# The second pass of the attention scores as two 64-row matmuls on different halves of the rows, with a second copy of the keys' high part

## The chip, the cores and the metric

The kernel runs on one core of a Trainium2 chip, in one launch. The metric is the device time of one execution in microseconds (us), as the median of several; less is better. The engines are named as in the profile: PE does matmuls (PEld its weight loads), DVE, ACT and POOL do elementwise work, and SP issues nearly all DMAs.

## The reference

One layer of a hybrid sequence model on 2048 tokens of width 1024. All three head groups read one projection of RMSNorm(x); their outputs are gated, concatenated, projected back and added to x, and a last RMSNorm follows. The change touches the first group, six heads of softmax attention over a band of nine 64-token chunks:

```python
scores = jnp.einsum('bnqhd,bnkhd->bnhqk', qc, kb).astype(jnp.float32) * (d ** -0.5)
...
scores = jnp.where(valid[None, :, None, None, :], scores + bias[None, None], NEG)
p = jax.nn.softmax(scores, axis=-1).astype(v.dtype)
o = jnp.einsum('bnhqk,bnkhd->bnqhd', p, vb)
```

Here d is 64. The second group is an mLSTM and the third a gated linear attention (GLA), both chunk by chunk with a carried state.

## The kernel before

**Numbers in two parts.** A float32 matmul operand is split into a high part, its value rounded to the type float32r, and a low part, the rest. A product is then made of float32r matmuls: high with high, high with low, low with high.

**Two stages.** Stage A goes through the tokens in four blocks of 512 (`q` = 0 to 3, `QT` = 512): projections (lines 243 to 245 and 263 to 265), mLSTM and GLA, and queries, keys and values of the attention written to DRAM (`q_d`, `k_d`, `v_d`) with the high and the low part side by side. Stage B, from `with ExitStack() as pb_` on, does the attention and the output projection for the same four blocks. The last few projections of stage A (`proj_kept`) are kept back and run in stage B, mixed with the attention of block 0. Then `load_wo` loads the output weights into the room that the projection weights leave, and from block 1 on the attention of block q is mixed with the output projection (`out_mm`, lines 945 to 947) of block q-1.

**Scores.** For each head, `scores` loads `qq` (L809, two DMAs: the queries' high and low part, each copied to rows 0 to 63 and to rows 64 to 127 of the 128 partitions, which are the rows of PE's array), `kk` (L812: the keys' high part on rows 0 to 63 and their low part on rows 64 to 127) and `vv` (L814). It then goes through four tiles of 128 queries (`tt`). A tile sees up to 640 keys, in at most two segments: up to 384 keys, and the last 256. Each segment has a PSUM bank of its own (`s`, two banks in all). L826 makes two passes over the segments: pass 0 multiplies the queries' high part, on both halves of the rows, with the whole of `kk`, and pass 1 the queries' low part in the same way. In block 0 the first two tiles have one segment only, and the others 128+256 and 256+256 keys; in blocks 1 to 3 every tile has 384+256. DVE reads a segment out of PSUM, adds the bias table `bt` or the mask `mz` and takes the minimum (L840), ACT does the exponential (L843), and POOL scales (L845).

**Mix.** `mix` transposes the probabilities on PE (L887), splits them (L892 on ACT, L893 on DVE), multiplies with `vv` (L901, L904), collects two heads in `cc` (L908 ACT, L909 DVE), multiplies with the gate `gt` (L921 POOL; loaded at L862) and splits the product (L852 ACT, L853 POOL).

**What sets the order.** PE's order is the order in which the code is written, as `merge` and `spread` interleave it. The other engines' and SP's order is set by the framework's scheduler. Each engine, and SP for its DMAs, takes its instructions in that order. A tile lives in a pool, at a fixed address; a tile in room that another tile used waits until that one's last reader and writer are done. The pool `early` of stage B lies at the right end of the on-chip memory. It holds `bt`, `bc`, `mz`, two `qq` and two `kk`, in this order from low to high addresses. It is opened after stage A's right-hand pools are closed, in room that these used. `bt` is loaded (L773), lowered by `bc` for each of the six heads (L777, POOL, six instructions) and partly overwritten (L778, POOL).

**Other 64-row matmuls.** Stage A has matmuls on 64 rows already: L522 multiplies six heads' keys with their queries in plain float32, the even heads on rows 0 to 63 and the odd ones on rows 64 to 127, into different banks. A plain float32 matmul is two instructions in the profile. The profile gives the part of the array that an instruction uses, rows*columns: 128*128 is the whole, 64*128 one half of the rows, 128*64 and 128*32 a part of the columns.

Of the kernel before, what the change touches and what calls it, by code (L numbers as in the profile page):

```python
# [8 lines left out]
FP32 = mybir.dt.float32  # L9
FR = mybir.dt.float32r  # L10
# [6 lines left out]
P = 128  # L17
D = 1024
KT = D // P
QT = 512  # L20
# [79 lines left out]
def f32(ap):  # L100
    return ap.bitcast(FP32)
# [3 lines left out]
def trunk_kernel(ctx: ExitStack, tc: tile.TileContext, xT, x, w_f, w_t, w_o, w_gates, norm_g, conv_w,  # L105
                 gate_sel, one_row, bias, ml_g, gla_g, final_g, out):
    nc = tc.nc
# [6 lines left out]
    k_d = dram.tile([AH, 2, 64, S], FP32, name="k_d")  # L114
# [27 lines left out]
    with ExitStack() as pa_:  # L142
# [3 lines left out]
        big = pa_.enter_context(tc.tile_pool(name="big", bufs=2, side="right"))  # L146
# [616 lines left out]
    with ExitStack() as pb_:  # L763
        psum = pb_.enter_context(tc.tile_pool(name="psumb", bufs=2, space=PSUM, reuse_waits="tile"))
        early = pb_.enter_context(tc.tile_pool(name="early", bufs=2, side="right", reuse_waits="tile"))
        big = pb_.enter_context(tc.tile_pool(name="bbig", bufs=2, side="right", reuse_waits="tile"))
        one = early

        def pbank(tag):
            return (psum_i if tag == "ip" else psum).tile([P, 512], FP32, name=tag)  # L770
# [29 lines left out]
        cur = {}  # L800

        def scores(q, h, out_):
            dma = nc.sync
            kb = max(0, q * QT - 512)
            nk = (q + 1) * QT - kb
            qq = early.tile([P, 2, QT], FR, name="qq")
            for r in range(2):
                a = h % 2
                dma.dma_start(f32(qq[64 * r:64 * r + 64]),  # L809
                                  q_d[h // 2, :, 64 * a:64 * a + 64, q * QT:(q + 1) * QT].rearrange("l d t -> d l t"))  # L810
            kk = early.tile([P, 1024], FR, name="kk")
            dma.dma_start(f32(kk[:, :nk]), k_d[h, :, :, kb:kb + nk].rearrange("l d t -> (l d) t"))  # L812
            vv = big.tile([P, 8, P], FR, name="vv", bufs=3)
            dma.dma_start(f32(vv[:, :nk // P, :]), v_d[h, kb:kb + nk, :].rearrange("(b p) d -> p b d", p=P))  # L814
            pts, pair = [], []
            for tt in range(NC):
                i = NC * q + tt
                k0 = max(0, i * P - 512)
                n = (i + 1) * P - k0
                ko = k0 - kb  # L820
                nA = max(0, n - 256)
                segs = ([(0, nA)] if nA else []) + [(nA, n - nA)]
                sps = [pbank("s") for _ in segs]
                for l in range(2):
                    for sp, (c0, cn) in zip(sps, segs):
                        nc.tensor.matmul(sp[:, :cn], qq[:, l, tt * P:(tt + 1) * P], kk[:, ko + c0:ko + c0 + cn],  # L826
                                         start=(l == 0), stop=(l == 1))
                if q == 0:
                    if tt < 2:
                        pair.append(big.tile([P, 640], FP32, name="pt", bufs=8))  # L830
                    pt = pair[(0, 1, 1, 0)[tt]]
                    pt = pt[:, (512, 384, 0, 0)[tt]:][:, 0:n]
                else:
                    pt = big.tile([P, 640], FP32, name="pt", bufs=8)
                sm = big.tile([P, 4], FP32, name="sm", bufs=8)
                init = -NEG
                for a, (sp, (c0, cn)) in enumerate(zip(sps, segs)):
                    last = a == len(segs) - 1
                    in1 = bt[:, h, 256 - cn:256] if last else mz[:, 384 - cn:384]
                    nc.vector.tensor_tensor_reduce(out=pt[:, c0:c0 + cn], in0=sp[:, :cn], in1=in1, scale=-1.0, scalar=init,  # L840
                                                   op0=ALU.add, op1=ALU.min, accum_out=sm[:, a:a + 1])
                    init = sm[:, a:a + 1]
                nc.scalar.activation(pt[:, :n], pt[:, :n], AF.Exp, bias=init, scale=-1.0, accum_out=sm[:, 2:3])  # L843
                nc.vector.reciprocal(sm[:, 3:4], sm[:, 2:3])  # L844
                nc.gpsimd.tensor_scalar(pt[:, :n], pt[:, :n], sm[:, 3:4], 0.5, op0=ALU.mult, op1=ALU.mult)  # L845
                pts.append((pt, ko // P, n // P))
                yield
            out_.append((vv, pts, nk // P))

        def split_y(src, k):  # L850
            yk = (big if k < 3 else late["p"]).tile([P, 2, QT], FR, name="y", bufs=6 if k < 3 else 5)
            nc.scalar.copy(yk[:, 0, :], src)  # L852
            nc.gpsimd.tensor_tensor(yk[:, 1, :], src, f32(yk[:, 0, :]), op=ALU.subtract)  # L853
            return yk

        def mix(q, h, Y, vv, pts, nkb):
            mr = slice(64 * (h % 2), 64 * (h % 2) + 64)
            cr = slice(64 - 64 * (h % 2), 128 - 64 * (h % 2))
            if h % 2 == 0:
                cur["cc"] = big.tile([P, QT], FP32, name="cc")  # L860
                cur["gt"] = big.tile([P, QT], FP32, name="gt")
                nc.sync.dma_start(cur["gt"], ga_d[:, h // 2, q * QT:(q + 1) * QT])  # L862
            cc, gt = cur["cc"], cur["gt"]
            todo = []
            for pr in range(NC // 2):
                pp = pts[2 * pr:2 * pr + 2]
                one_use, two_use = [], []
                for b in range(nkb):
                    use = tuple(tt for tt in range(2) if pp[tt][1] <= b < pp[tt][1] + pp[tt][2])
                    if use:  # L870
                        (one_use if len(use) == 1 else two_use).append((b, use))
                packs, width = [], 1024
                for b, use in one_use + two_use:
                    if width + P * len(use) > 512:
                        packs.append([])
                        width = 0
                    packs[-1].append((b, use, width))
                    width += P * len(use)
                todo += [(pr, pp, g, pk, g == len(packs) - 1) for g, pk in enumerate(packs)]
            ops = {}  # L880

            def turn_(pr, pp, g, pk, last):
                tp = pbank("tp")
                for b, use, w in pk:
                    for x_, tt in enumerate(use):
                        pt, b0, _ = pp[tt]
                        nc.tensor.transpose(out=tp[:, w + x_ * P:w + (x_ + 1) * P],  # L887
                                            in_=pt[:, (b - b0) * P:(b - b0 + 1) * P], identity=ident)
                wd = pk[-1][2] + P * len(pk[-1][1])
                ph = big.tile([P, 512], FR, name="ph", bufs=3)  # L890
                pl = big.tile([P, 512], FR, name="pl", bufs=3)
                nc.scalar.copy(ph[:, :wd], tp[:, :wd])  # L892
                nc.vector.tensor_tensor(pl[:, :wd], tp[:, :wd], f32(ph[:, :wd]), op=ALU.subtract)  # L893
                return ph, pl

            def pv(pr, pp, g, pk, last, ph, pl):
                if g == 0:
                    ops[pr] = pbank("w")
                op = ops[pr]
                for e, (b, use, w) in enumerate(pk):  # L900
                    nc.tensor.matmul(op[:, use[0] * P:use[0] * P + P * len(use)], vv[:, b, :], ph[:, w:w + P * len(use)],  # L901
                                     start=(g == 0 and e == 0), stop=False, skip_group_check=True)
                for e, (b, use, w) in enumerate(pk):
                    nc.tensor.matmul(op[0:64, use[0] * P:use[0] * P + P * len(use)], vv[:, b, 64 * (h % 2):64 * (h % 2) + 64],  # L904
                                     pl[:, w:w + P * len(use)], start=False, stop=(last and e == len(pk) - 1), skip_group_check=True)
                if last:
                    ps_ = slice(pr * ST, (pr + 1) * ST)
                    nc.scalar.copy(cc[mr, ps_], op[cr, :ST])  # L908
                    nc.vector.tensor_tensor(cc[mr, ps_], op[mr, :ST], cc[mr, ps_], op=ALU.add)  # L909

            held = []
            for it in todo:
                ph, pl = turn_(*it)
                yield
                if held:
                    pv(*held.pop())
                    yield
                held.append(it + (ph, pl))
            pv(*held.pop())
            if h % 2 == 1:  # L920
                nc.gpsimd.tensor_tensor(cc, cc, gt, op=ALU.mult)  # L921
                Y[h // 2] = split_y(cc, h // 2)
            yield
# [148 lines left out]
```

## Time and profile before

| | |
|---|---|
| median of 3 runs | 1430.01 us (1427.89 to 1431.16) |
| the profiled execution | 1430.58 us, of which 1428.9 us from its first to its last instruction |
| PE's mean granted clock | 0.953 of full speed |
| stage B | from 1005 us to the end |
| L826, all 360 matmuls | 80.8 us busy, 333 ns each as recorded |
| DMA traffic | 180.10 MB, 126 GB/s in the mean |

The rows that the argument rests on stand in the prediction. In a timeline row the first number is the start of the first instruction in us, the second the time from there to the end of the last one, and xN their number; [..] is idle time before it and who ended it. PE starts an instruction while those ahead of it still run, so what one costs is read from start to start and not from its recorded duration.

### The profile page before, as it was taken

What the parts mean: (1) busy time and instruction counts of PE and PEld (TensorE: products, weight loads), DVE (VectorE), ACT (ScalarE), POOL (GpSimd) and SP (SyncE); (2) the same over time, 40 slices, a digit from 0 to 9 for tenths busy, and PEclk for the clock granted to TensorE, in tenths of its full rate; (3) what the DMA queues carried; (4) which work ended last, traced back from release to release, by engine and by line L of the source; (5) the groups of instructions that cost most, each with busy time, mean ns of one, the idle gap of its engine ahead of it and who ended that gap; (6) DMA issues with size and microseconds to landing.
All of it is one profiled execution on the core that took longest, in us unless ns stands there. A gap on an engine that the chain in (4) does not pass through costs nothing.

```text
span 1428.9 us, 20086 instructions
## 1 busy us (share of the span) xinstructions
PE 1319.6 (92%) x7044; PEld 1064.9 (75%) x7044; DVE 788.7 (55%) x1874; ACT 616.5 (43%) x1173; POOL 606.5 (42%) x847
## 2 busy tenths in 40 slices
PE   5899989989998998999899899998878999999997
PEld 2678768867877876888677677787756887877876
DVE  6525556662664765265566527556556756656731
ACT  5634313463432347343224534321456555655531
POOL 4215762322576222266622325651245354454452
PEclk7999989999999999999999999997877999999999
DMA  7433214453421445432244533231587464555322
GB/s 245 152 112 117 74 54 131 133 177 111 118 74 56 130 140 177 125 111 74 67 124 121 156 118 93 73 110 49 148 241 229 130 184 133 179 161 160 99 67 89
DMA packets 107205, 180.10 MB, mean 126 GB/s; under 512 B 9824, under 2 KB 54752, under 8 KB 107104
## 3 DMA queue, kind: packets, MB, share of 16 engines
q1 hardware_dynamic: 102496, 170.43, 40.4%
q10 hardware_dynamic: 4608, 8.39, 1.6%
q8 instruction: 56, 0.92, 0.3%
q14 instruction: 45, 0.37, 0.1%
HBM read 143.14 MB, written 35.65 MB: 125 GB/s over the span
## 4 chain that ended last, share of the span: by engine, by line
PE 67%; DVE 12%; ACT 8%; DMA 6%; issue 4%; POOL 3%; SPq 0%; POOLq 0%; ACTq 0%; DVEq 0%
PE ip L243 11%; PE ip L245 10%; PE ip L244 10%; PE s L826 3%; PE ip L947 3%; PE ip L946 3%; PE ip L945 3%; PE ip L263 3%; PE ip L264 3%; PE ip L265 3%; PE tp L887 2%; DVE pt L840 2%; PE ga L673 2%; ACT w L235 2%; DVE qk L449 2%
## 5 line engine op out<-in xcount | busy, mean ns | idle before, releaser
L243 PE MATMUL ip<-x,w 128*128 128x512 f32 x800 | 326.7, 408 | 0.0
L244 PE MATMUL ip<-x,w 128*128 128x512 f32 x800 | 313.3, 392 | 1.2 <-DVE x L324 1.2
L245 PE MATMUL ip<-x,w 128*128 128x512 f32 x800 | 313.6, 392 | 0.0
L235 ACT CAST w<-wraw 128x1024 fp32r<-128x1024 f32 x132 | 138.3, 1049 | 193.9 <-PE ip L245 136.4
L236 DVE TENSOR_TENSOR w<-wraw,w 128x1024 fp32r<-128x1024 f32 x88 | 114.2, 1299 | 172.1 <-ACT w L235 170.0
L236 POOL TENSOR_TENSOR w<-wraw,w 128x1024 fp32r<-128x1024 f32 x44 | 106.1, 2410 | 217.5 <-ACT w L235 217.3
L243 PEld LDWEIGHTS ip<-x,w 128*128 128x128 f32 x800 | 150.9, 189 | 43.8 <-issue 11.9
L244 PEld LDWEIGHTS ip<-x,w 128*128 128x128 f32 x800 | 151.1, 189 | 32.8 <-DVE x L324 2.9
L245 PEld LDWEIGHTS ip<-x,w 128*128 128x128 f32 x800 | 150.7, 188 | 33.0
L845 POOL TENSOR_SCALAR pt<-pt,sm 128x640 f32<-128x640 f32 (+2 forms) x96 | 70.4, 735 | 148.8 <-DVE sm L844 118.1
L263 PE MATMUL ip<-w,x 128*128 128x512 f32 x256 | 105.5, 412 | 20.8 <-ACT zg L423 14.4
L264 PE MATMUL ip<-w,x 128*128 128x512 f32 x256 | 104.1, 407 | 4.6 <-POOL w L236 3.8
L945 PE MATMUL ip<-wo,y 128*128 128x512 f32 x256 | 107.0, 418 | 0.0
L843 ACT ACTIVATE pt<-pt,sm 128x640 f32<-128x640 f32 (+2 forms) x96 | 73.3, 764 | 71.0 <-DVE sm L840 68.0
L265 PE MATMUL ip<-w,x 128*128 128x512 f32 x256 | 103.3, 403 | 0.0
L947 PE MATMUL ip<-wo,y 128*128 128x512 f32 x256 | 101.7, 397 | 0.3 <-POOL y L853 0.3
L946 PE MATMUL ip<-wo,y 128*128 128x512 f32 x256 | 101.5, 396 | 0.0
L893 DVE TENSOR_TENSOR pl<-tp,ph 128x512 fp32r<-128x512 f32 (+2 forms) x126 | 74.6, 599 | 31.5 <-ACT ph L892 30.4
L826 PE MATMUL s<-kk,qq 128*128 128x384 f32 (+1 forms) x360 | 80.8, 333 | 10.7 <-DVE sm L840 9.2
L826 PEld LDWEIGHTS s<-kk,qq 128*128 128x128 f32 x360 | 60.6, 201 | 29.9 <-DVE sm L840 23.4
L633 POOL TENSOR_TENSOR prd<-gk,zg 128x16 f32<-128x16 f32 (+15 forms) x128 | 66.5, 520 | 33.4 <-PE pw L639 26.5
L892 ACT CAST ph<-tp 128x512 fp32r<-128x512 f32 (+2 forms) x126 | 63.1, 509 | 33.6 <-PE tp L887 32.4
(240 smaller groups left out, 2418.8 us busy)
## 6 DMA issues: line engine op xcount, KB each, us to landing
wraw<-in_w_f SPq DMA_DIRECT2D x100, 512.0 KB, 3.6
wraw<-in_w_t SPq DMA_DIRECT2D x32, 512.0 KB, 4.2
qq<-q_d SPq DMA_DIRECT2D x48, 256.0 KB, 4.5
kk<-k_d SPq DMA_DIRECT2D x18, 512.0 KB, 6.4
vv<-v_d SPq DMA_DIRECT2D x18, 512.0 KB, 7.3
xraw<-in_x SPq DMA_DIRECT2D x16, 512.0 KB, 4.6
xraw<-in_xT SPq DMA_DIRECT2D x16, 512.0 KB, 7.5
xr<-in_x SPq DMA_DIRECT2D x16, 512.0 KB, 3.7
```

Source lines behind the costliest of these rows:

```text
L235: nc.scalar.copy(w[:, :, 0, :], rv)
L236: other().tensor_tensor(w[:, :, 1, :], rv, f32(w[:, :, 0, :]), op=ALU.subtract)
L243: nc.tensor.matmul(ps, w[:, k, 0, :], X[k][:, 0, :], start=(k == 0), stop=False)
L244: nc.tensor.matmul(ps, w[:, k, 0, :], X[k][:, 1, :], start=False, stop=False)
L245: nc.tensor.matmul(ps, w[:, k, 1, :], X[k][:, 0, :], start=False, stop=(k == KT - 1))
L263: nc.tensor.matmul(ps, X[k][:, 0, t], w[:, 0, :], start=(k == 0), stop=False)
L264: nc.tensor.matmul(ps, X[k][:, 0, t], w[:, 1, :], start=False, stop=False)
L265: nc.tensor.matmul(ps, X[k][:, 1, t], w[:, 0, :], start=False, stop=(k == KT - 1))
L826: nc.tensor.matmul(sp[:, :cn], qq[:, l, tt * P:(tt + 1) * P], kk[:, ko + c0:ko + c0 + cn], start=(l == 0), stop=(l == 1))
L945: nc.tensor.matmul(ps, Y[k][:, 0, t], wo[k, j][:, 0, :], start=(e == 0), stop=False)
L946: nc.tensor.matmul(ps, Y[k][:, 0, t], wo[k, j][:, 1, :], start=False, stop=False)
L947: nc.tensor.matmul(ps, Y[k][:, 1, t], wo[k, j][:, 0, :], start=False, stop=(e == KT - 1))
```

## The change

`scores` loads a second copy of the keys' high part, `k2`, on rows 64 to 127 (L815), for the last 640 keys (512 in block 0). Pass 0 stays as it was (L829). In pass 1 (L833) only the keys' high part is multiplied with the queries' low part: the product of the two low parts is no longer made. The first segment uses rows 0 to 63 (`qq` and `kk`), the last segment rows 64 to 127 (`qq` and `k2`); a tile with one segment uses rows 64 to 127. `cc` and `gt` have one buffer each where they had two. Lines behind the change stand six lines further on than before (L840 is now L846, L945 is L951).

```diff
             kk = early.tile([P, 1024], FR, name="kk")
             dma.dma_start(f32(kk[:, :nk]), k_d[h, :, :, kb:kb + nk].rearrange("l d t -> (l d) t"))
+            kn = min(nk, QT + P)
+            k2 = early.tile([P, QT + P], FR, name="k2")[64:128]
+            dma.dma_start(f32(k2[:, :kn]), k_d[h, 0, :, kb + nk - kn:kb + nk])
...
-                for l in range(2):
-                    for sp, (c0, cn) in zip(sps, segs):
-                        nc.tensor.matmul(sp[:, :cn], qq[:, l, tt * P:(tt + 1) * P], kk[:, ko + c0:ko + c0 + cn],
-                                         start=(l == 0), stop=(l == 1))
+                ql = slice(tt * P, (tt + 1) * P)
+                for sp, (c0, cn) in zip(sps, segs):
+                    nc.tensor.matmul(sp[:, :cn], qq[:, 0, ql], kk[:, ko + c0:ko + c0 + cn], start=True, stop=False)
+                for e, (sp, (c0, cn)) in enumerate(zip(sps, segs)):
+                    r = slice(0, 64) if e < len(segs) - 1 else slice(64, 128)
+                    kx = kk[r, ko + c0:ko + c0 + cn] if e < len(segs) - 1 else k2[:, ko + c0 - nk + kn:ko + c0 + cn - nk + kn]
+                    nc.tensor.matmul(sp[:, :cn], qq[r, 1, ql], kx, start=False, stop=True)
...
-                cur["cc"] = big.tile([P, QT], FP32, name="cc")
-                cur["gt"] = big.tile([P, QT], FP32, name="gt")
+                cur["cc"] = big.tile([P, QT], FP32, name="cc", bufs=1)
+                cur["gt"] = big.tile([P, QT], FP32, name="gt", bufs=1)
```

On PE nothing else moves. In the middle of block 2 a tile of scores stands between `mix` and the output projection; before:

```order
L901 MATMUL w<-ph,vv 128x256
L904 MATMUL w<-pl,vv 64x256
L826 MATMUL s<-kk,qq 128x384
L826 MATMUL s<-kk,qq 128x256
L826 MATMUL s<-kk,qq 128x384
L826 MATMUL s<-kk,qq 128x256
L945 MATMUL ip<-wo,y 128x512
```

and now, with `k2` under a name with its number:

```order
L907 MATMUL w<-ph,vv 128x256
L910 MATMUL w<-pl,vv 64x256
L829 MATMUL s<-kk,qq 128x384
L829 MATMUL s<-kk,qq 128x256
L833 MATMUL s<-kk,qq 128x384
L833 MATMUL s<-k_10626,qq 128x256
L951 MATMUL ip<-wo,y 128x512
```

The four matmuls have the same columns as before; the last two are now on 64 rows each.

`early` grows by two tiles of 2,560 bytes a partition and so begins 5,120 bytes lower: `bt` is at byte 206,016 of each partition before and at 200,896 now, and reaches into the room of a GLA tile (`n`, up to byte 202,656) that stage A uses to its end. This moves the loads of `bt`, `bc` and of the first heads' `qq` and `kk`. On SP's queue they stood before in stage A's block 3, among its weight loads:

```order
L594 DMA y_d<-m 128x3x128
L233 DMA wraw<-in_w_t 128x1024
L773 DMA bt<-in_bias 128x6x256
L775 DMA bc<-in_bias 128x6x1
L809 DMA qq<-q_d 64x2x512
L233 DMA wraw<-in_w_t 128x1024
L809 DMA qq<-q_d 64x2x512
L812 DMA kk<-k_d 128x512
```

and now they stand behind the last store of the mLSTM's output, the last thing that stage A does:

```order
L724 DMA y_d<-n 128x2x128
L594 DMA y_d<-m 128x3x128
L773 DMA bt<-in_bias 128x6x256
L775 DMA bc<-in_bias 128x6x1
L809 DMA qq<-q_d 64x2x512 x2
L812 DMA kk<-k_d 128x512
L815 DMA k_8204<-k_d 64x512
L817 DMA vv<-v_d 128x4x128
```

Before, only `vv` and `gt` stood behind that store. POOL's work on `bt` moves with it: it was spread through the GLA of block 3, and is now one piece between the last mLSTM chunk and the first scaling of probabilities:

```order
L580 TENSOR_TENSOR sm<-sm 128x6
L780 MEMSET mz 128x384
L781 MEMSET mz 64x64
L777 TENSOR_SCALAR bt<-bt,bc 128x256 x6
L778 MEMSET bt 64x6x64
L851 TENSOR_SCALAR pt<-pt,sm 128x128
```

DVE's first reading of scores (L846, L840 before) now waits for that last MEMSET of `bt`. Further down SP's queue each head has one DMA more, `k2`, between `qq` and `vv`.

## The prediction

> **What bounds the kernel now.** I read the page first, then the busy time by stretches, then what PE waits for in the attention.
>
> ```profile
> span 1428.9 us, 20086 instructions
> PE 1319.6 (92%) x7044; PEld 1064.9 (75%) x7044; DVE 788.7 (55%) x1874; ACT 616.5 (43%) x1173; POOL 606.5 (42%) x847
> PE 67%; DVE 12%; ACT 8%; DMA 6%; issue 4%; POOL 3%; SPq 0%; POOLq 0%; ACTq 0%; DVEq 0%
> ```
>
> PE is busy for 92% and holds 67% of the chain that ended last. The change touches only stage B, so its stretches count (block 0 beside the kept projections, the loading of the output weights, and block 2):
>
> ```profile
> core 0: us, PE busy (x) PEld busy (x) DVE busy (x) ACT busy (x) POOL busy (x), PEclk, DMA share, GB/s
> 1003.00:1050.00 47.00, 44.02 (x254) 36.92 (x255) 28.00 (x113) 23.87 (x66) 14.12 (x25) 0.95 0.60 166
> 1050.00:1100.00 50.00, 36.44 (x144) 28.41 (x143) 27.57 (x71) 29.68 (x61) 26.57 (x24) 0.62 0.89 253
> 1187.00:1270.00 83.00, 79.50 (x492) 67.63 (x491) 55.60 (x164) 47.31 (x107) 31.61 (x35) 0.99 0.51 150
> ```
>
> The first and the last are PE's: 44 of 47 and 79.5 of 83 us. The middle one is the DMAs': their share is 0.89 while PE's clock falls to 0.62. What PE still waits for in blocks 1 to 3 (1100 to 1400 us) is mostly DVE's emptying of the two score banks and ACT's copy:
>
> ```profile
> PEld s L826 <- DVE sm L840: 15.1, 28, 1.4
> PEld w L904 <- DVE pl L893: 7.2, 20, 0.7
> PEld w L901 <- ACT ph L892: 6.7, 9, 1.1
> ```
>
> That is 29 us in all. So time added to PE's matmuls in the attention lands on the end, less what falls into these waits or under the DMAs of 1050 to 1100.
>
> **The second pass.** An undisturbed tile of scores in block 2 on PE's timeline:
>
> ```profile
> 1194.18 0.28 PE L901 MATMUL w<-ph,vv 128*128 128x256 f32 x1
> 1194.30 0.28 PE L904 MATMUL w<-pl,vv 128*64 128x256 f32 x1
> 1194.41 0.74 PE L826 MATMUL s<-kk,qq 128*128 128x384 f32 x4
> 1195.00 0.40 PE L945 MATMUL ip<-wo,y 128*128 128x512 f32 x1
> 1195.23 0.40 PE L946 MATMUL ip<-wo,y 128*128 128x512 f32 x1
> ```
>
> The four matmuls take 0.59 us from start to start for 1280 columns, so 256 columns take 0.59 x 256/1280 = 0.12. If the two matmuls of the new pass run side by side, the tile saves the shorter one: 0.12 us with 384+256 or 256+256 columns, 0.06 with 128+256. Whether they do, and what the way in and out costs, stage A shows: L522 has such pairs.
>
> ```profile
> 262.72 0.39 PE L244 MATMUL ip<-x,w 128*128 128x512 f32 x1
> 262.94 0.39 PE L245 MATMUL ip<-x,w 128*128 128x512 f32 x1
> 263.26 0.94 PE L522 MATMUL s<-qk 64*128 64x128 f32 x12
> 264.13 0.55 PE L526 MATMUL mt<-ident,qk 128*128 128x128 f32 x3
> ...
> 270.28 0.84 PE L540 MATMUL s<-Cbd,qk 128*128 128x130 f32 x6
> 270.96 1.45 PE L545 MATMUL s<-v,dd 128*128 128x65 f32 x12
> ```
>
> On the whole array (L540) six instructions of 130 columns take 0.68 us to the next line's start, 0.113 each. L522's twelve of 128 columns would take 12 x 0.111 = 1.34 one after another, and take 0.87; six pairs side by side would take 6 x 0.111 = 0.67. So they do run in pairs, and 0.20 us stand beside: the first pair's weights are loaded with nothing ahead to cover it, and the array empties behind the last pair. Before it there is more: L522 starts 0.32 behind L245, where L245 started 0.22 behind L244: 0.09 over the usual 0.23. The other instructions on part of the array show what follows behind:
>
> ```profile
> 272.33 0.57 PE L557 MATMUL mt<-v,m 128*64 128x65 f32 x12
> 272.83 0.50 PE L243 MATMUL ip<-x,w 128*128 128x512 f32 x1
> 273.17 0.39 PE L244 MATMUL ip<-x,w 128*128 128x512 f32 x1
> 273.40 0.40 PE L245 MATMUL ip<-x,w 128*128 128x512 f32 x1
> ```
>
> The first matmul behind takes 0.34 where the next takes 0.23: 0.11 for weights that could not be loaded ahead. So a visit to half the rows costs 0.09 + 0.20 + 0.11 = 0.40 us, against 0.12 saved. I take this although L904 above enters (0.12 behind L901) and leaves (0.11) a 128*64 form for nothing: in the built program L904 still addresses all groups of columns, while L833 addresses half the groups of rows, as L522 does. That L833 is float32r and L522 plain float32 is the doubt that is left.
>
> The Trainium skill speaks for the change and against it. "TensorE: Matmul & The Clock Gate", section "Part 3: Packing small matmuls", has matmuls on different row groups about 4 ns apart and no price for the switch; by it the sum below would be a gain (the third rival). "TensorEngine Tiling (Array Packing)", section "Key Properties", says that changing the tiling mode drains the engine, without a figure; the first page's "Step-by-step" puts a drain at about 128 cycles, 53 ns at 2.4 GHz. By that estimate, in and out at 53 ns for the 0.09 on each side here, the total would be some 6 us lower; the rows decide.
>
> Per tile: blocks 1 to 3 have 72 tiles of 384+256 columns, 0.40 - 0.12 = 0.28 each, 20.2 us. Block 0 has 12 tiles with one segment, 0.40 each, 4.8; six with 128+256, 0.34 each, 2.0; six with 256+256, 0.28 each, 1.7. Together 28.7 us of PE time. Of this, eight tiles of block 1 lie between 1070 and 1100, under the DMAs: 2.2 off. Block 0's first two are hidden in the late start (next part): 0.8 off. Of the other 25.7, part falls into waits: where two tiles follow each other the second waits for DVE, which gets the first's banks only some 0.2 us later, so little is hidden there; in front of L901 and L904 a tile of scores in between hides its own length. I take a fifth off: **+20.5 us**, between 13 (half hidden) and 28.
>
> **The late start.** At the change of stages:
>
> ```profile
> 1005.42 0.36 SPq L594 DMA_DIRECT2D y_d<-m  x1
> 1005.88 0.52 PE L826 MATMUL s<-kk,qq 128*128 128x128 f32 x2
> 1006.43 0.29 DVE L840 CUSTOM_DVE_ANT_0 pt<-s,bt 128x128 f32<-128x128 f32 x1 [1.04 <-PE s L826]
> 1008.59 0.62 PE L826 MATMUL s<-kk,qq 128*128 128x128 f32 x4
> ```
>
> Now `bt`, `bc`, `qq`, `kk` and `k2` are issued only behind that store. Their times to landing and POOL's work on `bt`:
>
> ```profile
> qq<-q_d SPq DMA_DIRECT2D x48, 256.0 KB, 4.5
> kk<-k_d SPq DMA_DIRECT2D x6, 256.0 KB, 5.4
> bt<-in_bias SPq DMA_DIRECT2D x1, 768.0 KB, 5.0
> bc<-in_bias SPq DMA_DIRECT2D x1, 3.0 KB, 4.7
> ...
> L777 POOL TENSOR_SCALAR bt<-bt,bc x6: 924/926/970, 803.3 to 808.7; 128x256 f32<-128x256 f32 x6
> ...
> L778 POOL MEMSET bt<- x1: 413/413/413, 811.0 to 811.0; 64x384 f32 x1
> ```
>
> `bt` goes out at about 1005.9 and is there at 1010.9; `bc`, issued some 0.6 later, at 1011.2. POOL then needs 6 x 0.926 + 0.41 = 6.0 us, to 1017.2, and only then DVE reads the first scores: 10.8 us later than at 1006.43. PE can do the first two tiles meanwhile (`kk`, fourth behind `bt` with some 0.6 us each, lands at about 1013.5, `k2` behind it), since there are two banks; the third tile, at 1008.59 before, must wait for both to be read, about 1018. **+9.5 us.** Nothing on PE can fill it: its order is fixed. Nothing gives it back either, since the kept projections end that much later, and the output weights' loads start from there. Bounds: 0 if the stretch to 1100 swallows it, 12 if `bt` takes as long beside other traffic as the slowest kind of load on the page's list (7.3 us).
>
> **DMA and buffers.** `k2` is 64 x 640 x 4 bytes, 0.16 MB a head, 0.13 in block 0. By SP's order three of block 1's fall into the DMA-bound stretch: 0.49 MB at 253 GB/s is **+2 us** there; elsewhere the DMAs have room (0.51 and 0.60). One buffer for `cc`:
>
> ```profile
> 1119.43 1.29 POOL L853 TENSOR_TENSOR y<-cc,y 128x512 fp32r<-128x512 f32 x1
> 1123.46 0.37 ACT L908 COPY cc<-w 64x256 f32<-64x256 f32 x1
> ```
>
> The next pair's first copy into `cc` (L908) comes 2.7 us behind the last reader (1120.7), so the wait is met already; in block 0 the two lie closer, and ACT may stand for 0 to 3 us, behind which its casts of the output weights queue. That is in the DMA-bound stretch; I take 0 and keep 3 for the range. A gate `gt` is read two heads after it is loaded. Cost nothing.
>
> **Sum.** 20.5 + 9.5 + 2 = +32 us on the profiled execution's 1430.58, of which 1428.9 is its span: 1462.6. The median of the runs is 0.6 lower, so **1462 us**. Its own range: +13 +7 +0 = 1450 to +28 +12 +5 = 1475.
>
> **Rivals.** (1) The visit costs what it did above, but the late start is swallowed by the DMA-bound stretch: 1462 - 9.5 = 1452. For it: PE has 14 us idle there. Against: the loads that bound it start only after the kept projections. Chance 0.08. (2) The change doesn't do what it says: the two halves run one behind the other, so the 0.12 a tile are not saved: 72 x 0.12 + 6 x 0.06 + 6 x 0.12 = 9.7 more, a fifth off, 1470. Against it are L522's pairs. Chance 0.08. (3) In float32r the visit is free, as L904's is, and the pairs do run together: 9.7 saved on PE, a fifth hidden, -7.8, and the late start and DMAs stay: 1430 - 7.8 + 11.5 = 1434. Chance 0.10. (4) The other side, faster: the same free visit, at each of the 96 tiles, at a price of -7.8; it decides the sign from the point where the late start and the DMAs cost less than 7.8 together, which they do if POOL's work on `bt` overlaps its landing or PE's queue recovers some 5 us before 1045: 1425. Chance 0.04.
>
> **Chances.** My forecast has 0.70. The measurement can tell about 0.2%, 2.9 us, from no change. Faster is rival 4, 0.04; within 0.2% is what of rival 3 lies under 1433, 0.04; slower is the rest, 0.92. The range leaves out rivals 3 and 4 and the forecast's outermost ends: 1443 to 1475.
>
> **What would show it.** Right: on PE's timeline an undisturbed tile in block 2 takes about 0.8 us from L829 to the next line's start less that line's own late weights (0.59 now), L833's two matmuls start within 0.01 us of each other, and the L951 behind takes 0.34 to L952's start; L846's first reading stands about 11 us behind the last `y_d<-m`, with L777's six in one piece ahead of it; block 2's stretch grows by some 5 us. Wrong: a tile of 0.47 us (the visit is free), of 0.9 (no pairs), or a first L846 near 1007.

## The result and the profile after

The changed kernel takes **1464.12 us** (median of 4 runs, 1461.45 to 1467.87) against 1430.24 before, a ratio of 1.0242 (95% interval 1.0221 to 1.0264). It is slower; forecast were 1462 us and a range of 1443 to 1475. The profiled execution took 1462.41 us. Of all executions reported below one is left out: the profiled one of the first run with two visits a tile, 2374 us where its three others took 1466 to 1474.

First the page's span and busy times of the changed kernel:

```profile
span 1460.7 us, 20105 instructions
PE 1346.6 (92%) x7044; PEld 1061.5 (73%) x7044; DVE 791.0 (54%) x1874; ACT 616.2 (42%) x1173; POOL 609.5 (42%) x847
```

PE has as many matmuls as before and is busy 27 us longer; the other engines' busy time has hardly moved. Where the 31.8 us came from is read from stretches that hold the same work. Before, these were 1003 to 1050, 1050 to 1100, 1100 to 1187 and 1187 to 1270 us; the third of them was not shown so far:

```profile
1100.00:1187.00 87.00, 83.36 (x489) 70.19 (x488) 56.76 (x165) 48.22 (x110) 42.14 (x43) 0.99 0.56 161
```

In the changed kernel the same PE instructions lie here (columns: length, then PE, PEld, DVE, ACT and POOL busy, PE's clock, DMA share, GB/s):

```profile
1004.50:1068.50 64.00, 53.65 (x255) 39.76 (x255) 28.18 (x113) 24.12 (x67) 19.97 (x31) 0.83 0.70 169
1068.50:1116.60 48.10, 34.19 (x145) 23.71 (x144) 27.15 (x71) 28.77 (x60) 26.23 (x24) 0.72 0.95 256
1116.60:1207.40 90.80, 88.38 (x486) 68.41 (x486) 56.42 (x165) 48.73 (x111) 42.95 (x44) 0.98 0.69 173
1207.40:1294.60 87.20, 84.66 (x491) 66.04 (x491) 55.65 (x164) 47.01 (x107) 31.60 (x35) 0.98 0.60 152
```

Block 0 beside the kept projections is 17 us longer (64 for 47), the DMA-bound stretch 1.9 shorter, and the two stretches of the attention beside the output projection are 3.8 and 4.2 longer. What is left to the end takes 166.1 us (from 1294.6) where it took 158.9 (from 1270), 7.2 longer, and stage B begins 1.5 later. These make the 31.8.

**The way in and out of the half rows**, on PE's timeline of an undisturbed tile in block 2:

```profile
1215.72 0.45 PE L829 MATMUL s<-kk,qq 128*128 128x384 f32 x2
1216.10 0.44 PE L833 MATMUL s<-kk,qq 64*128 64x384 f32 x1
1216.11 0.38 PE L833 MATMUL s<-k,qq 64*128 64x256 f32 x1
1216.47 0.50 PE L951 MATMUL ip<-wo,y 128*128 128x512 f32 x1
1216.81 0.40 PE L952 MATMUL ip<-wo,y 128*128 128x512 f32 x1
```

The two matmuls of L833 start within 0.01 us, so they do run side by side. From L829 to L951 it is 0.75 us where it was 0.59, and L951 takes 0.34 to the next line where it took 0.23: 0.27 us more for the tile, though 256 columns fewer stream. The weight loads of the same tile show why:

```profile
1215.61 0.30 PEld L829 LDWEIGHTS s<-kk,qq 128*128 128x128 f32 x2
1216.10 0.18 PEld L833 LDWEIGHTS s<-kk,qq 64*128 64x128 f32 x1 [0.19 <-issue]
1216.10 0.18 PEld L833 LDWEIGHTS s<-k,qq 64*128 64x128 f32 x1
1216.46 0.19 PEld L951 LDWEIGHTS ip<-wo,y 128*128 128x128 f32 x1 [0.18 <-issue]
```

L829's weights are loaded 0.11 us ahead of their matmul (1215.61 and 1215.72). L833's and L951's are loaded only when the array changes its form, with PEld idle 0.19 and 0.18 before them and no engine to wait for ("issue"). Summed over 1100 us to the end, the waits ahead of weight loads are (engine, tile, line, what was waited for: us in total, times, longest):

```profile
PEld s L829 <- DVE sm L846: 13.5, 25, 2.6
PEld s L833 <- issue: 9.5, 48, 0.3
PEld w L910 <- DVE pl L899: 7.8, 21, 1.1
PEld w L907 <- ACT ph L898: 7.1, 12, 1.0
PEld ip L951 <- issue: 6.2, 34, 0.2
PEld tp L893 <- issue: 3.1, 15, 0.3
PEld w L907 <- issue: 2.2, 12, 0.2
```

The "issue" rows are new: 21 us that stood in no list before. They are time of the weight loads; part of it lies beside matmuls that still run. The rows with a named releaser are 28.4 us together, where those of before (shown in the prediction) were 29, so ahead of the weight loads the waits for DVE and ACT hardly shrank. What counts for the path is what PE itself waits, and that did shrink, as the kernel with the visits alone shows below.

**The late start**, on the timeline of the changed kernel at the change of stages:

```profile
1006.00 0.36 SPq L594 DMA_DIRECT2D y_d<-m  x1
...
1009.24 0.59 SPq L812 DMA_DIRECT2D kk<-k_d  x1
...
1012.79 5.46 POOL L777 TENSOR_SCALAR bt<-bt,bc 128x256 f32<-128x256 f32 x6 [8.46 <-DMA bc<-in_bias]
...
1016.24 0.45 PE L829 MATMUL s<-kk,qq 128*128 128x128 f32 x1 [9.58 <-DMA kk<-k_d]
...
1018.76 0.29 DVE L846 CUSTOM_DVE_ANT_0 pt<-s,bt 128x128 f32<-128x128 f32 x1 [12.78 <-POOL bt L778]
```

The six of L777 stand in one piece, and DVE reads 12.8 us after the store where it read 1.0 after it before. But PE stands first, and for another reason: its first matmul waits 9.58 us for `kk` and starts 7.0 us after the issue of that load. From there on PE is busy without a gap up to the third tile's first matmul and beyond it, which the prediction had waiting for the table:

```profile
1020.76 0.63 PE L829 MATMUL s<-kk,qq 128*128 128x128 f32 x2
```

### The profile page after: what moved, and what is told of

Same layout as the page of the kernel before. It is cut to its first block, busy times and chain, and to the rows that moved or that the text cites. A ratio compares the mean times of both kernels' runs of the same rounds, so it can differ in the third digit from the quotient of the medians.

```text
span 1460.7 us, 20105 instructions
## 1 busy us (share of the span) xinstructions
PE 1346.6 (92%) x7044; PEld 1061.5 (73%) x7044; DVE 791.0 (54%) x1874; ACT 616.2 (42%) x1173; POOL 609.5 (42%) x847
## 4 chain that ended last, share of the span: by engine, by line
PE 68%; DVE 10%; ACT 8%; DMA 7%; issue 4%; POOL 3%; SPq 0%; POOLq 0%; ACTq 0%; DVEq 0%
PE ip L243 11%; PE ip L245 10%; PE ip L244 10%; PE ip L951 3%; PE ip L953 3%; PE ip L952 3%; PE ip L264 3%; PE ip L263 3%; PE ip L265 3%; PE tp L893 3%; PE s L833 2%; PE s L829 2%; PE ga L673 2%; ACT w L235 2%; PE w L910 2%
## 5 line engine op out<-in xcount | busy, mean ns | idle before, releaser
L244 PE MATMUL ip<-x,w 128*128 128x512 f32 x800 | 314.1, 393 | 1.3 <-DVE x L324 1.3
L245 PE MATMUL ip<-x,w 128*128 128x512 f32 x800 | 314.3, 393 | 0.0
L244 PEld LDWEIGHTS ip<-x,w 128*128 128x128 f32 x800 | 151.7, 190 | 32.8 <-DVE x L324 2.9
L245 PEld LDWEIGHTS ip<-x,w 128*128 128x128 f32 x800 | 151.3, 189 | 33.2
L951 PE MATMUL ip<-wo,y 128*128 128x512 f32 x256 | 111.1, 434 | 0.0
L953 PE MATMUL ip<-wo,y 128*128 128x512 f32 x256 | 101.6, 397 | 0.3 <-POOL y L859 0.3
L952 PE MATMUL ip<-wo,y 128*128 128x512 f32 x256 | 101.5, 396 | 0.0
L449 DVE SCALAR_TENSOR_TENSOR qk<-u,cw,qk 128x512 f32<-128x512 f32 x72 | 67.5, 938 | 17.9 <-ACT qk L447 15.8
L263 PEld LDWEIGHTS ip<-w,x 128*128 128x128 f32 x256 | 50.4, 197 | 34.4 <-ACT zg L423 16.2
```

The source lines that it names most:

```text
L244: nc.tensor.matmul(ps, w[:, k, 0, :], X[k][:, 1, :], start=False, stop=False)
L245: nc.tensor.matmul(ps, w[:, k, 1, :], X[k][:, 0, :], start=False, stop=(k == KT - 1))
L263: nc.tensor.matmul(ps, X[k][:, 0, t], w[:, 0, :], start=(k == 0), stop=False)
L951: nc.tensor.matmul(ps, Y[k][:, 0, t], wo[k, j][:, 0, :], start=(e == 0), stop=False)
L952: nc.tensor.matmul(ps, Y[k][:, 0, t], wo[k, j][:, 1, :], start=False, stop=False)
L953: nc.tensor.matmul(ps, Y[k][:, 1, t], wo[k, j][:, 0, :], start=False, stop=(e == KT - 1))
```

## The experiments

Theory: three costs add up, some 20 us for the visits, 9.5 for the late start and 2 for the loads of `k2`. Rivals: the late start is swallowed; the loads cost and not the visits; the pairs do not pay or get in each other's way.

Stage A is the same code in all kernels, and yet its last store goes out between 1000.80 and 1013.34 us in the profiled executions. So beside each ratio stands, from the profile, the time from the start of the last `y_d<-m` to the end of the span, with the difference to the kernel before. Before it is 1428.9 - 1005.42 = 423.5 us. The span and the store of the kernel with the visits alone, which has the earliest, 1447.7 - 1000.80 = 446.9:

```profile
span 1447.7 us, 20086 instructions
1000.80 0.36 SPq L594 DMA_DIRECT2D y_d<-m  x1
```

and the latest store, in the kernel with two visits a tile (second run):

```profile
1013.34 0.36 SPq L594 DMA_DIRECT2D y_d<-m  x1
```

| kernel | median, us | ratio to before (95%) | store to end, us |
|---|---|---|---|
| changed | 1464.12 | 1.0242 (1.0221 to 1.0264) | 454.7 (+31.2) |
| visits alone | 1451.13 | 1.0157 (1.0127 to 1.0188) | 446.9 (+23.4) |
| late start alone | 1438.73 | 1.0060 (1.0036 to 1.0085) | 431.8 (+8.4) |
| both segments on the same half | 1458.85 | 1.0198 (1.0169 to 1.0227) | 449.0 (+25.5) |
| second copy in another pool | 1457.41 | 1.0188 (1.0161 to 1.0214) | 452.1 (+28.7) |
| two visits a tile, second run | 1472.45 | 1.0301 (1.0264 to 1.0339) | 466.7 (+43.2) |
| pairs issued twice | 1464.80 | 1.0240 (1.0220 to 1.0261) | 454.0 (+30.5) |
| late start and unread copy | 1458.49 | 1.0183 (1.0155 to 1.0211) | 453.2 (+29.8) |
| one buffer for `cc`, `gt` | 1428.23 | 0.9984 (0.9971 to 0.9998) | 419.8 (-3.7) |
| late start and loads | 1440.96 | 1.0074 (1.0049 to 1.0099) | 433.5 (+10.1) |

The medians of the kernel before beside these were 1430.24 us (changed), 1429.67 (the four rows below it), 1430.52 (two visits a tile, second run; late start and loads) and 1431.02 (the other three). The last column rests on one execution of each kernel. One buffer for `cc` and `gt` alone stands at -3.7 in it, so differences of up to some 4 us in it say nothing.

**The visits alone.** Edit to the kernel before:

```diff
-                for l in range(2):
-                    for sp, (c0, cn) in zip(sps, segs):
-                        nc.tensor.matmul(sp[:, :cn], qq[:, l, tt * P:(tt + 1) * P], kk[:, ko + c0:ko + c0 + cn],
-                                         start=(l == 0), stop=(l == 1))
+                ql = slice(tt * P, (tt + 1) * P)
+                for sp, (c0, cn) in zip(sps, segs):
+                    nc.tensor.matmul(sp[:, :cn], qq[:, 0, ql], kk[:, ko + c0:ko + c0 + cn], start=True, stop=False)
+                for e, (sp, (c0, cn)) in enumerate(zip(sps, segs)):
+                    r = slice(0, 64) if e < len(segs) - 1 else slice(64, 128)
+                    kx = kk[r, ko + c0:ko + c0 + cn]
+                    nc.tensor.matmul(sp[:, :cn], qq[r, 1, ql], kx, start=False, stop=True)
```

> The kernel before with only the second pass changed: each tile's first segment on rows 0 to 63 and its last segment on rows 64 to 127, and no second copy of the keys. The last segment's second pass takes the keys' low part instead of the high part, because that is what lies on rows 64 to 127; nothing else is changed, so neither the late start nor a new load is there. My theory (each visit to half the rows costs 0.40 us and saves 0.12, four fifths of it on the path): +20 us, 1450 (13 to 28 more). Rival A, from the gap between the two kernels' traces, where only 15 us grow behind 1102 us and some 6 of these stand where the clock falls at the starts of blocks 2 and 3: the visits proper are worth +10 to +14, 1442, and the rest comes with the loads of the second copy and the late start. Rival B (the visit is free and the pairs save): -8, 1422.

Measured 1451.13: the theory's 1450, not rival A's 1442. The tile is the changed kernel's (0.75 us to L948):

```profile
1202.95 0.45 PE L826 MATMUL s<-kk,qq 128*128 128x384 f32 x2
1203.34 0.44 PE L830 MATMUL s<-kk,qq 64*128 64x384 f32 x2
1203.70 0.50 PE L948 MATMUL ip<-wo,y 128*128 128x512 f32 x1
```

and of the four stretches with the same work as above, the first and the last are here:

```profile
999.30:1053.20 53.90, 53.23 (x255) 39.73 (x255) 27.59 (x112) 24.00 (x67) 13.99 (x24) 0.89 0.53 149
...
1194.00:1281.80 87.80, 85.23 (x492) 66.67 (x492) 55.69 (x164) 46.88 (x107) 31.58 (x35) 0.97 0.47 141
```

So with the visits alone the first stretch grows by 6.9 us and the last one by 4.8, where the changed kernel has 17.0 and 4.2. The clock is lower in both (0.89 for 0.95 and 0.97 for 0.99), so the growth is not all the visits' own time; the last section comes back to this.

PE's own waits for DVE and ACT from 1003 us on come to 26.2 us before and to 21.6 here. The rows of before, beside 9.2 for L840 (shown below) and 0.8 for L844, and then all of this kernel's:

```profile
PE w L901 <- ACT ph L892: 12.6, 13, 5.9
PE w L904 <- DVE pl L893: 3.6, 8, 1.0
```

```profile
PE w L904 <- ACT ph L895: 10.1, 12, 5.3
PE s L826 <- DVE sm L843: 8.2, 18, 0.8
PE w L907 <- DVE pl L896: 3.3, 6, 1.2
```

So 4.6 us of the visits fell into these waits.

**The late start alone.** Edit to the kernel before:

```diff
+        pad = one.tile([P, 2 * (QT + P)], FP32, name="pad", bufs=1)
         late = {}
...
-                cur["cc"] = big.tile([P, QT], FP32, name="cc")
-                cur["gt"] = big.tile([P, QT], FP32, name="gt")
+                cur["cc"] = big.tile([P, QT], FP32, name="cc", bufs=1)
+                cur["gt"] = big.tile([P, QT], FP32, name="gt", bufs=1)
```

> The kernel before with one buffer for the gate and for the two heads' sum, and a tile of 5120 bytes a partition that nobody uses in the pool of the bias table. The table then lies in the room of the GLA tile as in the changed kernel and is loaded after stage A. No visit to half the rows, no second copy of the keys. My theory: the late start alone, +9.5 us, 1440; the first reading of scores stands some 11 us behind the last store of the mLSTM. Rival (the late start is swallowed by the stretch behind it, where the DMAs are the bound): 0 to +3, 1431 to 1433.

Measured 1438.73, +9.1 us. The first two stretches of this kernel:

```profile
1005.60:1062.90 57.30, 45.79 (x254) 38.14 (x255) 27.46 (x112) 23.59 (x67) 19.97 (x31) 0.84 0.69 173
1062.90:1111.60 48.70, 32.95 (x144) 25.52 (x143) 27.83 (x72) 29.15 (x61) 26.05 (x24) 0.68 0.90 247
```

The first grows by 10.3 us, the DMA-bound one gives back 1.3: not swallowed. With the visits' 6.9 the first makes 17.2, where the changed kernel has 17.0.

**Both segments on the same half.** Edit to the kernel with the visits alone:

```diff
-                    r = slice(0, 64) if e < len(segs) - 1 else slice(64, 128)
+                    r = slice(0, 64)
```

> As the kernel with the visits alone, but both segments' second pass stands on rows 0 to 63, so that they cannot run side by side. The last segment's second pass then takes the keys' high part on rows 0 to 63, so nothing but the product of the two low parts is left out. My theory: the visit's 0.40 us per tile with nothing saved: 9.7 us of PE time more than with the pairs, some 8 on the path, 1458. Rival (the visit costs because the two matmuls get in each other's way when they run together, in writing or in reading): the same as with the pairs or less.

Measured 1458.85, as the theory has it. An undisturbed tile:

```profile
1214.56 0.46 PE L826 MATMUL s<-kk,qq 128*128 128x384 f32 x2
1214.95 0.55 PE L830 MATMUL s<-kk,qq 64*128 64x384 f32 x2
1215.43 0.51 PE L948 MATMUL ip<-wo,y 128*128 128x512 f32 x1
```

It takes 0.87 us to L948, 0.12 more than with the pairs: the pair saves just what the shorter matmul's columns take. What that is worth on the path is less sure. The medians are 7.7 us apart, with intervals that overlap, and from the store to the end the two profiled executions differ by 2.1 only, which is within the noise of that column.

**The second copy in another pool.** Edit to the changed kernel:

```diff
-            k2 = early.tile([P, QT + P], FR, name="k2")[64:128]
+            k2 = big.tile([P, QT + P], FR, name="k2")[64:128]
```

> The changed kernel with the second copy of the keys in the pool of the probabilities instead of the pool of the bias table. The bias table keeps the place and the early load that it has before the change; the first second copy is still loaded behind stage A's last store. My theory: the visits (+20.5) and the loads (+2) stay, and of the late start some 4.5 us are left, since PE's first second pass waits about that long for its keys: 1457, 5 us under the changed kernel's. Rival A (the late start is swallowed anyway): no difference from the changed kernel, 1464. Rival B (the loads of the second copy are what costs, not the visits): as rival A, and the kernel with the visits alone is near 1435.

Measured 1457.41. The bias table and the first keys are early again, and PE's first tile waits only for `k2`:

```profile
1007.27 0.47 PE L833 MATMUL s<-k,qq 64*128 64x128 f32 x1 [3.46 <-DMA k<-k_d]
```

By the medians, each beside its own kernel before, the change costs 27.7 us with this placement where it cost 33.9, and the two intervals of the ratios do not overlap. From the store to the end the gain is 2.5, within the noise of that column. The kernel stays slower than the one before, as the visits do.

**Two visits a tile.** Edit to the kernel with the visits alone:

```diff
-                for sp, (c0, cn) in zip(sps, segs):
+                for e, (sp, (c0, cn)) in enumerate(zip(sps, segs)):
                     nc.tensor.matmul(sp[:, :cn], qq[:, 0, ql], kk[:, ko + c0:ko + c0 + cn], start=True, stop=False)
-                for e, (sp, (c0, cn)) in enumerate(zip(sps, segs)):
                     r = slice(0, 64) if e < len(segs) - 1 else slice(64, 128)
```

> As the kernel with the visits alone (the last segment's second pass with the keys' low part), but written as first segment on the whole array, first segment on half the rows, last segment on the whole array, last segment on half the rows. A tile with two segments now goes to half the rows twice, and nothing runs side by side; the columns are the same. My theory, with the size that the traces of the first four kernels show for an undisturbed visit with nothing saved (0.39 us from the first matmul of the tile to the second behind it): the price is for each way in and out, so 0.78 us a tile, 72 x 0.78 + 12 x 0.78 + 12 x 0.39 = 70 us gross, five sixths of it on the path, +59, 1489. Rival (the price belongs to the second pass as such, its weights of 64 rows or its sums on half the array, and not to the change of form): 0.39 a tile as in the kernel with both on the same half, 1459.

Measured 1473.06 (ratio 1.0283, 1.0255 to 1.0311): neither the 1489 of the theory nor the 1459 of the rival. It ran once more for a profile that can be set beside the others:

> The kernel with two visits a tile again, for a profile that can be set beside the others: the first one's profiled execution had PE's matmuls slow from beginning to end, 2374 us. My theory after the first one's 1473 us: an undisturbed tile is 0.78 us longer than before, but the last segment's first matmul now stands behind a visit, so its bank is free by then and more of the price falls into waits. Rival (the second visit of a tile is cheaper than the first): an undisturbed tile is longer by clearly less than 0.7 us.

Measured 1472.45. An undisturbed tile now:

```profile
1247.84 0.34 PE L826 MATMUL s<-kk,qq 128*128 128x384 f32 x1
...
1249.09 0.50 PE L947 MATMUL ip<-wo,y 128*128 128x512 f32 x1
1249.43 0.39 PE L948 MATMUL ip<-wo,y 128*128 128x512 f32 x1
```

From the tile's first matmul to L948 it is 1.59 us, before 0.59 + 0.23 = 0.82: 0.77 more, twice the 0.39 of one visit without a saving. The price is for each way in and out. The theory misses on the path because more of it is covered: PE's own waits for DVE ahead of L826 are 1.4 us in two pieces from 1003 us on, and 9.2 in 24 before. The first row is this kernel's, the second the one before's:

```profile
PE s L826 <- DVE sm L842: 1.4, 2, 1.0
```

```profile
PE s L826 <- DVE sm L840: 9.2, 24, 1.0
```

These 8 us are half of what the theory was too high by; the rest was not traced.

**Pairs issued twice.** Edit to the kernel with the visits alone (the second line indents the loop's body):

```diff
-                for e, (sp, (c0, cn)) in enumerate(zip(sps, segs)):
+                for g in range(2):
+                  for e, (sp, (c0, cn)) in enumerate(zip(sps, segs)):
...
-                    nc.tensor.matmul(sp[:, :cn], qq[r, 1, ql], kx, start=False, stop=True)
+                      nc.tensor.matmul(sp[:, :cn], qq[r, 1, ql], kx, start=False, stop=(g == 1))
```

> As the kernel with the visits alone, but the pair of the second pass is issued twice, so that the product with the queries' low part counts twice. One visit a tile, two pairs in it. My theory: the second pair costs only its longer stream, 384 columns at 0.59/1280 us each = 0.18 us, since the form of the array is not changed: 0.27 + 0.18 = 0.45 us a tile over the kernel before, and 72 x 0.18 + 6 x 0.18 x 128/384 + 18 x 0.12 = 15 us gross over the kernel with the visits alone, some 12 on the path, 1463. Rival (each pair pays for weights that can't be loaded ahead, and that is most of the visit's price): 0.27 + 0.18 + 0.2 = 0.65 us a tile, some 30 us more, 1478 or above.

Measured 1464.80. An undisturbed tile:

```profile
1230.99 0.46 PE L826 MATMUL s<-kk,qq 128*128 128x384 f32 x2
1231.38 0.61 PE L831 MATMUL s<-kk,qq 64*128 64x384 f32 x4
1231.91 0.50 PE L949 MATMUL ip<-wo,y 128*128 128x512 f32 x1
```

It takes 0.92 us to L949, 0.17 more than with one pair: a second pair in the same visit costs its longer stream (384 columns are 0.18) and nothing else. By the medians the kernel costs 12.3 us more than with one pair, where the theory had 12.

**The late start with the loads.** Edit to the changed kernel: the second pass is the old one (as the removed lines of the visits' diff), and `k2` is loaded but not read.

> The changed kernel with the second pass as it was before the change, on all 128 rows with the keys' high and low part. The second copy of the keys is loaded but not read, and the pools are as in the changed kernel: the late start and the new loads without the visits. My theory: +9.1 (the late start as measured alone) and +2 for the loads, 1441. Rival (the loads cost more than I gave them, since they lie in the stretch where the DMAs are the bound and each head's first matmul waits behind one transfer more): +14 or more, 1444. Other rival (the loads hide altogether): 1439.

Measured 1458.49, a miss by 17 us, and of the experiment's own making. Nothing reads `k2`, so SP's queue runs ahead with its loads, each behind the last one into the same buffer:

```profile
1025.47 7.48 SPq L815 DMA_DIRECT2D k<-k_d  x5
1033.00 1.25 SPq L809 DMA_DIRECT2D qq<-q_d  x2
```

The next `qq` stands behind five of them, and PE waits for keys a second time (20.1 us in two pieces, of which 10.4 are the late start's):

```profile
PE s L829 <- DMA kk<-k_d: 20.1, 2, 10.4
```

Mended, with `k2` as operand of a full second pass:

```diff
+        k2s = [one.tile([P, QT + P], FR, name="k2" + c, bufs=1) for c in "ab"]
+        for k2 in k2s:
+            nc.gpsimd.memset(f32(k2[0:64]), 0.0)
...
-            k2 = early.tile([P, QT + P], FR, name="k2")[64:128]
-            dma.dma_start(f32(k2[:, :kn]), k_d[h, 0, :, kb + nk - kn:kb + nk])
+            k2 = k2s[h % 2]
+            dma.dma_start(f32(k2[64:128, :kn]), k_d[h, 0, :, kb + nk - kn:kb + nk])
...
-                    r = slice(0, 64) if e < len(segs) - 1 else slice(64, 128)
-                    kx = kk[r, ko + c0:ko + c0 + cn] if e < len(segs) - 1 else k2[:, ko + c0 - nk + kn:ko + c0 + cn - nk + kn]
-                    nc.tensor.matmul(sp[:, :cn], qq[r, 1, ql], kx, start=False, stop=True)
+                    kx = kk[:, ko + c0:ko + c0 + cn] if e < len(segs) - 1 else k2[:, ko + c0 - nk + kn:ko + c0 + cn - nk + kn]
+                    nc.tensor.matmul(sp[:, :cn], qq[:, 1, ql], kx, start=False, stop=True)
```

> The late start and the new loads without the visits, mended: in the run without the visits above nobody read the second copy, so its loads ran ahead on SP's queue, each waiting for the one before it, and held the queries' loads back. Here the second copy is the last segment's operand in a second pass on all 128 rows, with zeros on its rows 0 to 63, written once; it is loaded and freed at the places of the changed kernel. Of the computation only the product of the two low parts is left out, for the last segment. My theory: +9.1 (the late start as measured alone) and 0 to +2 for the loads, 1440. Rival (the loads cost much, as the unmended run's 1458 would have it): 1450 or above.

Measured 1440.96: 2.2 us above the late start alone by the medians (1.4 when each is set beside its own kernel before), 1.7 from the store to the end. The loads cost about what the theory gave them; the two intervals overlap, so that they cost nothing is not excluded.

**One buffer.** Edit to the kernel before: the `cc` and `gt` lines of the late start's diff alone.

> The kernel before with one buffer for the gate and one for the two heads' sum, and nothing else changed. My theory: nothing to be measured, 1430 (0 to 1.6 us more; in the changed kernel's trace PE waits once for the copy into the sum, 1.6 us, in the stretch where the DMAs are the bound). Rival (ACT's casts of the output weights queue behind the waiting copy): +3, 1433.

Measured 0.9984 of the time before (0.9971 to 0.9998): no cost. If anything it is a little faster, by less than the 0.2% that the prediction took as the least that can be told.

## Why the prediction was right

**The price of a visit** was forecast as 0.09 + 0.20 + 0.11 = 0.40 us from plain-float32 matmuls of stage A. In the changed kernel's tile it is: L829 to L833 0.38 where 640 columns take 0.295, so 0.09 in; L833 to L951 0.37 where 384 columns take 0.18, so 0.19 with the first weights and the emptying; and 0.11 behind L951. That is 0.39, and 0.27 a tile with the 0.12 that the pair saves (forecast 0.28). The doubt that float32r might change form for nothing, as L904's 128*64 does, is settled for the half rows: it pays. Why L904 does not, no run here shows; the prediction's reason for it was not tested. Two visits and doubled pairs show that it is a price per change of form and not per matmul. The Trainium skill's rule that a change of the tiling mode drains the engine ("TensorEngine Tiling (Array Packing)", section "Key Properties") agrees with the idle PEld on both sides (0.19 and 0.18 us). The estimate that the prediction worked out from the Trainium skill's "TensorE: Matmul & The Clock Gate", section "Step-by-step", 0.053 us for the way in, does not agree: the way in took 0.09.

**The share on the path** came out as forecast, in part by luck. With the visits alone the first two tiles are not hidden, so the forecast for them is four fifths of 28.7 - 2.2, or 21.2 us. Measured are 21.5 by the medians and 23.4 from the store to the end. At the measured prices the visits are 27.7 us in all, 25.5 without the eight tiles in the DMA-bound stretch, and PE's own waits swallowed 4.6 of them, close to the fifth. But the prediction left out the clock. With the visits it is at half speed for longer at the start of stage B, for some 3.6 us (estimate, last section), and without these it is some seven tenths of the visits that landed. Block 2 agrees: its 24 tiles of 0.27 us are 6.5, and its stretch grew by 4.8 and 4.2. What swallowed the rest was not traced.

**The late start** has its size (9.1 measured, 9.5 forecast) but not its mechanism, and that the two agree is luck. I had PE wait for DVE at the third tile, until the bias table is ready and both banks are read. PE did not wait there: its waits for DVE ahead of L829 are 0.2 us in all up to 1070 us. It stood at the first tile for its keys. I let `kk` land at about 1013.5, 8.1 us behind the store, and PE got it 10.2 us behind the store, since the load was issued a little later than I had it and took 7.0 us where the page's median was 5.4. The third tile then came 11.6 us later behind the store than before, with PE busy at half its clock from the first tile on. So block 0's first two visits were not hidden either, as I had them. The load stands behind the bias table's 768 KB on SP's queue; whether that made it slow was not tested, and moving it ahead of the table's was not tried. The second-copy-elsewhere kernel shows the same from the other side: with the table and the first keys early, 3.46 us of waiting are left.

**The loads and the buffers**: 2 forecast, 1.4 to 2.2 measured, within noise; one buffer costs nothing, forecast so.

**The rivals.** Swallowed late start (1452): only 1.3 us are given back. No pairs (1470): they start within 0.01 us, and apart they cost 0.12 a tile more. Free visit (1434, and 1425 on the other side): each visit costs 0.39. Of the prediction's own signs, the tile (0.75 us for about 0.8), the pair's start and L951's 0.34 came as told; DVE's first reading stood 12.8 us behind the store for 11, and block 2 grew by 4.2 us for 5.

The sum of the parts measured alone, 21.5 for the visits and 10.4 for late start and loads, is 31.9 us, and the change measures 33.9 (31.6 to 37.8 by its interval).

## What to carry to other kernels

Packing two half-row matmuls pays by the columns of the shorter one, and cost 0.39 us at full clock for each way into the half-row form and back, however many pairs stood in between (one or two here). Here a visit would have had to carry more than three pairs of 384+256 columns (3.3 x 0.12) where it carried one. In a profile the cost stands as PEld idle with "issue" as releaser on both sides of a changed form, not as a wait for anyone. Where a kernel has such forms already, as stage A's L522, their price can be read before packing more. And look where a grown pool pushes its first tile: 5 KB more a partition moved the loads of a table and of the first queries and keys over a stage's end, for 9 us that have nothing to do with the matmuls.

## What the runs showed of the hardware beside that

PE's clock is at half speed when stage B begins, ahead of any late load: L244 and L245, 512 columns each, start 0.43 us apart there in the changed kernel (1005.60 and 1006.03) as in the one before (1005.02 and 1005.45), and 0.23 at full speed. How long this lasts is not the same. From L591's matmul, where PE takes up work at the end of stage A, full speed is back after some 4 us in the kernel before (1003.92 to 1007.9) and 4.5 with one buffer. With the visits alone it takes some 11 us (999.30 to 1010.7), 11 to 12 with both segments on the same half and with pairs issued twice, and 15 with two visits a tile. Behind the late start's wait it takes some 10 us in the changed kernel and 4 to 6 in the three without visits; in the kernel with the second copy in another pool, which has visits, it is 5 behind its wait of 3.46.

So changes of form went along with a longer time at half clock in all of these kernels but the last; why was not tested. Some 7 us more at half speed are some 3.6 us of lost time (an estimate), of the 6.9 by which the visits alone lengthen the first stretch. The first stretch's mean clock is 0.95 before, 0.89 with the visits alone, 0.84 with the late start alone and 0.83 in the changed kernel.
